# Storing each output of the last macro tile but one in two DMAs with 8 KB reads, in a rot90 kernel on Trainium2

## The chip, the cores and the metric

The kernel runs on one core of one Trainium2 chip. The metric is the device time of one execution in microseconds (us). Runs are compared with runs of the same rounds on the same chip. A run's time is about 1.8 us longer than the span that its trace covers.

Names: a *macro tile* is 1024 x 4096 floats of the input (16 MB). There are 16, so *tile 15* is the last but one and *tile 16* the last. Each is loaded by eight DMAs of 2 MB and leaves as eight *outputs* of 2 MB, numbered 0 to 7. *The turn* is the passage from the last load and the last output of tile 15 to the first output of tile 16. (MB and KB: 2 MB is 2,097,152 bytes; GB/s, and MB with a decimal point, are decimal.)

Engines, as this kernel uses them: PE transposes, DVE and ACT copy, SP issues the loads and ACT the stores. SBUF is the memory of the tiles; PSUM is the one that PE writes its results to. A *landing* is the end of a DMA, an *issue* the instruction that starts it.

## The reference

```python
def setup_inputs():
    return {"x": np.random.randn(8192, 8192).astype(np.float32), "k": 1}

def reference(x, k):
    return np.rot90(x, k)
```

268.4 MB are read and 268.4 MB are written. Nothing is computed; the work is to move and to turn.

## The kernel before

A load brings 128 rows x 4096 columns into SBUF. DVE reverses the columns inside each 128-wide block while copying to the reversal buffers `ar` (68 of them; one macro tile fills 64). PE transposes the 128 x 128 blocks into PSUM, 32 for one output, in two halves of 16. ACT copies each half to an output buffer `ot`, and issues the store. Pools: two load buffers, two output buffers, two PSUM tiles (each half an output).

```python
    a_pool = ctx.enter_context(tc.tile_pool(name="a_pool", bufs=2))
    r_pool = ctx.enter_context(tc.tile_pool(name="r_pool", bufs=68))
    o_pool = ctx.enter_context(tc.tile_pool(name="o_pool", bufs=2))
    psum_pool = ctx.enter_context(
        tc.tile_pool(name="psum", bufs=2, space=bass.MemoryType.PSUM)
    )
    # ... loads (SP queue) and DVE reversals, then for each output of the tile:
            if last and g0 // G % 2 == 0:
                ot = a_pool.tile([P, W], dt, tag="a")   # load buffers are free by then
            else:
                ot = o_pool.tile([P, W], dt, tag="o")
            o = ot.rearrange("m (g f) -> m g f", g=G)   # G = 4
            S = PW if last and g0 + G == C // P else G  # PW = 2
            for h in range(0, G, PW):
                ps = psum_pool.tile([P, PW, R], mybir.dt.float32)
                # ... 16 transposes into ps
                nc.scalar.copy(o[:, G - PW - h : G - h, :], ps[:])
                done = h + PW
                if done % S == 0:
                    # ... dst: S blocks of 128 rows x 1024 columns of out
                    nc.scalar.dma_start(out=dst, in_=o[:, G - done : G - done + S, :])
```

After scheduling, `whole_reads` rewrites the SBUF side of every store into one contiguous read for each partition. A 2 MB store thus reads 16 KB at a time, like a load. (Its HBM side still writes rows of 4 KB.) The profile shows these pieces as packets: it counts 144 for a 2 MB DMA, 18432 for the 128 loads, one for each of the 128 pieces and 16 of under 512 B (4112 of these in all 257 DMAs).

```python
                if len(ap) == 3 and ap[2][0] == 1 and ap[1][0] == ap[2][1]:
                    ap = [ap[0], [1, 1], [1, ap[1][1] * ap[2][1]]]
```

Of the kernel before, what the change touches and what calls it, by code (L numbers as in the profile page):

```python
# [2 lines left out]

# [5 lines left out]

P = 128  # L10




R = 1024
RT = R // P
LAST = [4096]
W = 4096
CH = 512
G = 4  # L20
PW = 2


def whole_reads(nc):






    for fn in nc.m.functions:
        for block in fn.blocks:
            for n, ins in enumerate(block.instructions):
                if not isinstance(ins, mybir.InstDMACopy):
                    continue
                src = ins.ins[0]
                ap = [list(d) for d in src.ap]
                if len(ap) == 3 and ap[2][0] == 1 and ap[1][0] == ap[2][1]:
                    ap = [ap[0], [1, 1], [1, ap[1][1] * ap[2][1]]]
                    block.instructions[n] = copy.replace(  # L40
                        ins,
                        ins=[copy.replace(src, ap=ap)],
                        ant_dge_precooked=False,
                    )


def macro_tiles(N, M):

    for r0 in range(0, N, R):
        widths = [W] * (M // W)  # L50
        if r0 + R == N:
            widths[-1:] = LAST
        c0 = 0
        for C in widths:
            yield r0, c0, C
            c0 += C


@with_exitstack
def kernel(  # L60
    ctx: ExitStack,
    tc: tile.TileContext,
    x: bass.AP,
    k: bass.AP,
    out: bass.AP,
):
    nc = tc.nc
    assert k == 1, f"only k=1 supported, got {k}"
    nc.at_finalize(whole_reads)

    N, M = x.shape
    dt = x.dtype

    consts = ctx.enter_context(tc.tile_pool(name="consts", bufs=1))
    ident = consts.tile([P, P], dt)
    make_identity(nc, ident)
# [8 lines that stand above are left out]
    tiles = list(macro_tiles(N, M))  # L85
    loads = 0
    for r0, c0, C in tiles:
        last = (r0, c0, C) == tiles[-1]
        q = W // C
        chunks = {}  # L90
        for t0 in range(0, RT, q):


            if loads < RT and loads % 4 >= 2:
                a = o_pool.tile([P, W], dt, tag="o")
            else:
                a = a_pool.tile([P, W], dt, tag="a")
            loads += 1
            a = a.rearrange("r (q c) -> r q c", q=q)
            nc.sync.dma_start(  # L100
                out=a,
                in_=x[r0 + t0 * P : r0 + (t0 + q) * P, c0 : c0 + C].rearrange(
                    "(q r) c -> r q c", q=q
                ),
            )


            for u in range(q):
                for j in range(C // CH):
                    ar = r_pool.tile([P, CH // P, P], dt, tag="ar")  # L110
                    nc.vector.tensor_copy(  # L111
                        out=ar[:],
                        in_=a[:, u, j * CH : (j + 1) * CH].rearrange(
                            "r (b m) -> r b m", m=P
                        )[:, :, ::-1],
                    )
                    chunks[t0 + u, j] = ar

        for g0 in range(0, C // P, G):

            if last and g0 // G % 2 == 0:
                ot = a_pool.tile([P, W], dt, tag="a")
            else:
                ot = o_pool.tile([P, W], dt, tag="o")
            o = ot.rearrange("m (g f) -> m g f", g=G)
            S = PW if last and g0 + G == C // P else G
            for h in range(0, G, PW):
                ps = psum_pool.tile([P, PW, R], mybir.dt.float32)
                for w in range(PW):
                    g = g0 + h + w  # L130
                    for t in range(RT):
                        nc.tensor.transpose(  # L132
                            ps[:, PW - 1 - w, t * P : (t + 1) * P],
                            chunks[t, g * P // CH][:, g % (CH // P), :],
                            ident,
# [5 lines that stand above are left out]
                    top = M - c0 - (g0 + done) * P  # L141
                    dst = out[top : top + S * P, r0 : r0 + R].rearrange(
                        "(g m) f -> m g f", g=S
                    )
                    nc.scalar.dma_start(  # L145
                        out=dst, in_=o[:, G - done : G - done + S, :]
                    )


# [1 line left out]
_INS = ['x', 'k']  # L151
_OUTS = [((8192, 8192), 'float32')]

_NUMBERS = {'k': 1}


# [26 lines left out]
```

## Time and profile before

| | before |
|---|---|
| time, median (lowest to highest) | 1271.75 us (1271.64 to 1271.89), 4 runs |
| span of the trace | 1269.2 us |
| PE / ACT / DVE busy | 56% / 37% / 28% |
| DMA, mean | 424 GB/s |

These lines are from the page of the profile: the busy tenths of the DMA engines and the rate, in 40 equal slices of the span; the chain that ended last, by line; and the DMA issues, with the median time from issue to landing as the last number.

```profile
...
DMA  9999999999999999999999999999999999999989
GB/s 400 415 431 429 429 428 429 430 428 429 428 429 428 430 430 428 429 429 430 428 428 420 429 429 429 429 429 427 428 422 427 426 421 430 427 427 427 428 342 382
...
DMA out_dram<-ot 72%; ACT ot L137 18%; DMA a<-in_x_dram 6%; DVE ar L111 1%; PE ps L132 1%; ACTq L145 0%; ACTq L137 0%; DVEq L111 0%
...
a<-in_x_dram SPq DMA_DIRECT2D x128, 2048.0 KB, 16.8
out_dram<-ot ACTq DMA_DIRECT2D x127, 2048.0 KB, 15.8
...
```

Nine tenths and more in every slice but one, at some 429 GB/s in most: the DMA engines bound the kernel. The slices that fall off are the last two. The timeline shows why. Its columns are start, duration, engine and line, operation, and in brackets how long the engine had been idle and what ended that; `x2` means that a line merges two instructions, and its duration runs from the start of the first to the end of the last. L137 is the ACT copy, L145 the store, L111 the DVE reversal, L132 the transposes.

```profile
...
1202.12 3.63 ACT L137 COPY ot<-ps 128x2048 f32<-128x2048 f32 x2 [6.19 <-DMA out_dram<-ot]
...
1211.95 3.63 ACT L137 COPY ot<-ps 128x2048 f32<-128x2048 f32 x2 [6.19 <-DMA out_dram<-ot]
...
1215.62 0.55 ACTq L145 DMA_DIRECT2D out_dram<-ot  x1
1218.09 2.77 DVE L111 COPY ar<-a 128x512 f32<-128x512 f32 x8 [7.05 <-DMA a<-in_x_dram]
...
1218.57 6.39 PE L132 MATMUL ps<-ident,ar 128*128 128x128 f32 x41 [3.72 <-DVE ar L111]
1220.79 1.87 ACT L137 COPY ot<-ps 128x2048 f32<-128x2048 f32 x1 [5.20 <-PE ps L132]
1223.25 1.87 ACT L137 COPY ot<-ps 128x2048 f32<-128x2048 f32 x1 [0.60 <-PE ps L132]
1225.15 0.55 ACTq L145 DMA_DIRECT2D out_dram<-ot  x1
...
```

The pace is 9.83 us for an output (1202.12 to 1211.95) as long as loads and stores run side by side. Then the last load lands and is reversed from 1218.09 on, and its transposes and the two ACT copies end at 1225.12. The first store of tile 16 is issued at 1225.15, when the last store of tile 15 (issued at 1215.62) is nearly out. The table of five-microsecond stretches of the same trace shows the hole. After the length come the busy us (and instructions) of PE, its weight loads, DVE, ACT and POOL; the last three columns are the granted TensorE clock, the busy share of the DMA engines, and GB/s.

```profile
...
1210.00:1215.00 5.00, 0.98 (x7) 0.74 (x7) 1.04 (x4) 3.05 (x2) 0.00 (x0) 1.00 0.90 382
1215.00:1220.00 5.00, 1.43 (x7) 1.43 (x8) 1.91 (x6) 0.59 (x1) 0.00 (x0) 0.53 0.80 338
1220.00:1225.00 5.00, 4.96 (x36) 4.72 (x34) 0.86 (x3) 3.61 (x2) 0.00 (x0) 0.79 0.34 144
1225.00:1230.00 5.00, 4.25 (x37) 3.97 (x38) 0.00 (x0) 3.76 (x3) 0.00 (x0) 1.00 0.74 315
...
```

Against 430 GB/s, these four stretches lose (48 + 92 + 286 + 115) x 5 / 430 = 6.3 us of transfer time. The change aims at this hole.

### The profile page before, as it was taken

Reading aid. Unit: us, or ns where it says so; the run is one execution under the profiler, and the core shown is the slowest. Engines: PE = TensorE matmul, PEld = TensorE weight load, DVE = VectorE, ACT = ScalarE, POOL = GpSimd, SP = SyncE. Lnnn points to the kernel's source line nnn. Section 1 sums busy time; section 2 is a strip of 40 time slices with the busy share of each in tenths; the row PEclk is TensorE's granted clock in tenths of the full one; section 3 lists DMA queues with packets and bytes.
Section 4 is the critical chain, followed back from the end, with each engine's and each line's share of the span. In section 5 each row is a group of like instructions: output and inputs, shape, how many; then the busy total and the mean of one; then the engine's idle time right before and its main releaser. Section 6 shows DMA issues by size and latency. Waiting matters only on the chain.

```text
span 1269.2 us, 10385 instructions
## 1 busy us (share of the span) xinstructions
PE 708.7 (56%) x4096; PEld 668.1 (53%) x4096; DVE 355.2 (28%) x1024; ACT 467.2 (37%) x257; POOL 0.7 (0%) x6
## 2 busy tenths in 40 slices
PE   1465645655556555665566555564555555655564
PEld 0364545645555455554556545554555555545564
DVE  4422322232223222232223222332223322232210
ACT  0333334333433343333433333333433343333454
POOL 0000000000000000000000000000000000000000
PEclk9968687776777867767767677677676877768787
DMA  9999999999999999999999999999999999999989
GB/s 400 415 431 429 429 428 429 430 428 429 428 429 428 430 430 428 429 429 430 428 428 420 429 429 429 429 429 427 428 422 427 426 421 430 427 427 427 428 342 382
DMA packets 37057, 537.55 MB, mean 424 GB/s; under 512 B 4112, under 2 KB 4112, under 8 KB 4112
## 3 DMA queue, kind: packets, MB, share of 16 engines
q10 hardware_dynamic: 18576, 268.44, 49.8%
q1 hardware_dynamic: 18432, 268.44, 49.8%
q8 instruction: 32, 0.52, 0.2%
q14 instruction: 17, 0.14, 0.0%
HBM read 268.44 MB, written 268.44 MB: 423 GB/s over the span
## 4 chain that ended last, share of the span: by engine, by line
DMA 78%; ACT 18%; DVE 1%; PE 1%; issue 1%; ACTq 0%; DVEq 0%
DMA out_dram<-ot 72%; ACT ot L137 18%; DMA a<-in_x_dram 6%; DVE ar L111 1%; PE ps L132 1%; ACTq L145 0%; ACTq L137 0%; DVEq L111 0%
## 5 line engine op out<-in xcount | busy, mean ns | idle before, releaser
L132 PE MATMUL ps<-ident,ar 128*128 128x128 f32 x4096 | 708.7, 353 | 544.3 <-ACT ot L137 461.5
L132 PEld LDWEIGHTS ps<-ident,ar 128*128 128x128 f32 x4096 | 668.1, 188 | 584.6 <-ACT ot L137 492.4
L137 ACT COPY ot<-ps 128x2048 f32<-128x2048 f32 x256 | 465.9, 1869 | 747.0 <-DMA out_dram<-ot 724.2
L111 DVE COPY ar<-a 128x512 f32<-128x512 f32 x1024 | 355.2, 421 | 865.7 <-DMA a<-in_x_dram 731.6
L137 ACT ACT_TABLE_LOAD x1 | 1.3, 1283 | 41.1 <-DVE ar L111 41.1
masks.py:199 POOL TENSOR_SCALAR_AFFINE_SELECT ident<-ident 128x128 f32<-128x128 f32 x1 | 0.3, 292 | 0.1
masks.py:197 POOL MEMSET ident<- 128x128 f32 x1 | 0.2, 204 | 0.3 <-POOLq L164 0.3
L164 POOL MEMSET const-bfloat16-1.0<- 128x1 bf16 x1 | 0.1, 101 | 0.0
L164 POOL MEMSET const-uint8-127<- 128x1 uint8 x1 | 0.1, 101 | 0.0
L164 POOL MEMSET const-float32-0.0<- 128x1 f32 x1 | 0.1, 98 | 0.2 <-issue 0.2
L164 POOL MEMSET const-float32-1.0<- 128x1 f32 x1 | 0.1, 98 | 0.0
## 6 DMA issues: line engine op xcount, KB each, us to landing
a<-in_x_dram SPq DMA_DIRECT2D x128, 2048.0 KB, 16.8
out_dram<-ot ACTq DMA_DIRECT2D x127, 2048.0 KB, 15.8
out_dram<-ot ACTq DMA_DIRECT2D x2, 1024.0 KB, 12.6
```

Of the source, the lines that this page charges most:

```text
L111: nc.vector.tensor_copy(out=ar[:], in_=a[:, u, j * CH : (j + 1) * CH].rearrange("r (b m) -> r b m", m=P)[:, :, ::-1],)
L132: nc.tensor.transpose(ps[:, PW - 1 - w, t * P : (t + 1) * P], chunks[t, g * P // CH][:, g % (CH // P), :], ident,)
L137: nc.scalar.copy(o[:, G - PW - h : G - h, :], ps[:])
L164: nc = _bacc.Bacc("TRN2", target_bir_lowering=False, num_devices=1)
```

## The change

The intent: give the loads of tile 16 a larger share of the DMA engines while tile 15 is being stored, so that they land early and the stores left over fill the hole.

```diff
+        ahead = (r0, c0, C) == tiles[-2]
...
-            S = PW if last and g0 + G == C // P else G
+            S = PW if ahead or (last and g0 + G == C // P) else G
```

The diff also removes the list `LAST = [4096]`, which had no effect. Each output of tile 15 now leaves in two 1 MB DMAs, whose SBUF reads are 8 KB instead of 16.

More of the change, by code (lines that the diff above doesn't have):

```diff
@@ L16 @@
 RT = R // P
-LAST = [4096]
 W = 4096
@@ L50, in macro_tiles @@
         widths = [W] * (M // W)
-        if r0 + R == N:
-            widths[-1:] = LAST
         c0 = 0
```

## The prediction

> **What bounds the kernel now.** The DMA engines. The page's forty slices show them 90% busy or more in all but one, at 427 to 430 GB/s in most; PE is busy 56%, ACT 37%, DVE 28%. 536.9 MB at 430 GB/s are 1249 us of the 1269 us span. The chain of waits shows the lockstep: landing of a store (15.8 us), two ACT copies (3.64 us), next store; with two output and two input buffers a 2 MB load and a 2 MB store pass in each 9.83 us.
>
> The change can reach only the loss at the turn into the last macro tile. In the timeline the last load's DVE copies start at 1218.1 us, the last store of the tile before is issued at 1215.6, and the first store of the last tile only at 1225.15, because transposes and two ACT copies lie between. The table of five-microsecond stretches from 1210 us shows 382, 338, 144, 315, 416 GB/s instead of 430: about 6.4 us of lost transfer time. The drain at the end (about 3 us) stays.
>
> **What the change does.** The eight 2 MB stores of the last macro tile but one become sixteen 1 MB stores with 8 KB SBUF reads. In the instruction order both halves are issued after the second ACT copy, so nothing starts earlier; eight more issues of 0.55 us fall on ACT, mostly in its waits. Bytes are the same; packets rise by about 1,150. [...] Then loads (16 KB) get two thirds and these stores (8 KB) one third. The trace of before shows no such share; it only mixes equal packets. So the last tile's loads run ahead of the stores, and the stores left over fill the gap while the last tile's first transposes and copies run.
>
> **How much comes back.** Not all. The last four chunks of each load need reversal buffers freed by the transposes of the matching output group (68 buffers, 64 in use), and these wait for ACT and so for slower stores. So the loads gain about one load's time: the last lands near 1209 instead of 1218 us. Then stores run alone with two buffers: between a landing and the next store's first bytes lie 3.64 us of ACT and about 3 us of latency (estimate: the first load landed at 8.1 us, where 2 MB at 430 GB/s take 4.9), more than the 4.9 us that the other buffer's 2 MB last. So a new dip of some 2 us opens. The last store of the tile before is issued near 1219 instead of 1215.6, the first of the last tile near 1223 instead of 1225. Stepping these durations through gives 1.5 us saved; the measured gap is deeper than in that sketch, so I say 2.2. [...]
>
> **Prediction: 1269.6 us**, 1266.0 to 1272.8. Chances: faster 0.01, within 2% 0.98, slower 0.01.
>
> **What would show it.** Issue to landing of the last eight loads falls from 16.8 to about 11 us at its shortest, and grows for the half stores. DVE then waits for PE in that tile. The dip of 144 GB/s at 1220 to 1225 us is partly filled, and another appears 5 to 10 us earlier. Before 1140 us nothing changes.
>
> **What would make it wrong.** Engines that share by bytes or by DMA, not by packets: no gain. A costly 8 KB packet: slower by 1 to 3 us. Loads held back less than I think: up to 5 us gained. [...]

The forecast of 1269.6 us is before's 1271.75 us less the 2.2 us saved. The shares were the author's assumption; they were measured afterwards (286 and 146 GB/s, below).

## The result

| | before | after |
|---|---|---|
| time, median (lowest to highest) | 1271.75 us (1271.64 to 1271.89) | 1271.47 us (1270.91 to 1271.85) |
| ratio, 95% interval | | 0.9997 (0.998 to 1.0015) |
| first store of tile 16 issued | 1225.15 us | 1226.09 us |
| time of the profiled run | 1270.97 us | 1271.85 us |

A ratio is the mean time of one kernel's runs over that of the other's of the same rounds, so it is not quite the ratio of the medians quoted. The time is the same within the noise. The time of 1271.47 lies in the predicted range, but that range (1266.0 to 1272.8) holds "no gain" as well as a gain, so this says little; the 2.2 us that were to come did not.

The page of the changed kernel, the lines that answer to those of before:

```profile
...
GB/s 398 415 432 429 428 429 428 430 428 429 428 429 430 428 429 428 428 429 430 429 429 426 426 429 427 428 429 427 428 426 428 425 426 429 428 426 413 395 368 382
...
DMA out_dram<-ot 47%; DMA a<-in_x_dram 31%; ACT ot L137 13%; DVE ar L109 5%; PE ps L132 1%; ACTq L145 0%; ACTq L137 0%; DVEq L109 0%
...
a<-in_x_dram SPq DMA_DIRECT2D x128, 2048.0 KB, 16.8
...
out_dram<-ot ACTq DMA_DIRECT2D x18, 1024.0 KB, 13.5
```

There are now 18 stores of 1 MB (two before), and the last four slices, not the last two, fall off. The timeline of tile 15's stores (ACT) and tile 16's loads (DVE; the reversal is L109 here):

```profile
...
1153.03 3.63 ACT L137 COPY ot<-ps 128x2048 f32<-128x2048 f32 x2 [6.26 <-DMA out_dram<-ot]
...
1157.68 2.77 DVE L109 COPY ar<-a 128x512 f32<-128x512 f32 x8 [5.52 <-DMA a<-in_x_dram]
1165.00 2.77 DVE L109 COPY ar<-a 128x512 f32<-128x512 f32 x8 [4.55 <-DMA a<-in_x_dram]
1167.77 3.63 ACT L137 COPY ot<-ps 128x2048 f32<-128x2048 f32 x2 [11.11 <-DMA out_dram<-ot]
...
1172.36 1.43 DVE L109 COPY ar<-a 128x512 f32<-128x512 f32 x4 [4.58 <-DMA a<-in_x_dram]
...
1182.11 3.63 ACT L137 COPY ot<-ps 128x2048 f32<-128x2048 f32 x2 [10.71 <-DMA out_dram<-ot]
...
```

Loads now land 7.3 us apart (1157.68, 1165.00, 1172.36), which is 2.10 MB / 7.34 us = 286 GB/s, two thirds of 430. Before it was one in 9.83 us. Outputs go the other way: ACT's waits for a store to land end 14.7 and 14.3 us apart (1153.03, 1167.77, 1182.11), 2.10 / 14.34 = 146 GB/s, one third. On average over this stretch the predicted share is there. The `x4` and the later groups of the same kind show DVE stopping half way through a load. Waits from 1140 us on (engine and tile, what it waited for, total us, times, longest), first before:

```profile
...
DVE ar L111 <- DMA a<-in_x_dram: 56.5, 8, 7.1
...
```

and after:

```profile
...
DVE ar L109 <- DMA a<-in_x_dram: 34.1, 7, 7.2
DVE ar L109 <- PE ps L132: 21.6, 5, 7.6
...
```

Before, DVE waited for loads alone. After, 21.6 us of its waiting is for PE to free reversal buffers: the loads have run as far ahead as they can. Now the turn, after:

```profile
...
1210.36 1.43 DVE L109 COPY ar<-a 128x512 f32<-128x512 f32 x4 [2.99 <-DMA a<-in_x_dram]
1211.59 3.63 ACT L137 COPY ot<-ps 128x2048 f32<-128x2048 f32 x2 [8.59 <-DMA out_dram<-ot]
...
1213.51 8.09 PE L132 MATMUL ps<-ident,ar 128*128 128x128 f32 x48 [6.84 <-ACT ot L137]
1217.22 1.86 ACT L137 COPY ot<-ps 128x2048 f32<-128x2048 f32 x1 [2.00 <-PE ps L132]
...
1219.88 1.87 ACT L137 COPY ot<-ps 128x2048 f32<-128x2048 f32 x1 [0.80 <-PE ps L132]
1219.94 2.38 ACTq L145 DMA_DIRECT2D out_dram<-ot  x2
...
1222.42 3.63 ACT L137 COPY ot<-ps 128x2048 f32<-128x2048 f32 x2 [0.67 <-ACT ot L137]
...
1226.09 0.55 ACTq L145 DMA_DIRECT2D out_dram<-ot  x1
...
```

and the stretches of the same trace:

```profile
...
1210.00:1215.00 5.00, 1.49 (x7) 1.49 (x8) 1.43 (x4) 3.41 (x2) 0.00 (x0) 0.50 0.70 295
1215.00:1220.00 5.00, 5.00 (x30) 5.00 (x29) 0.88 (x3) 2.21 (x3) 0.00 (x0) 0.61 0.96 398
1220.00:1225.00 5.00, 4.21 (x37) 3.74 (x36) 0.55 (x2) 4.33 (x3) 0.00 (x0) 1.00 0.82 338
1225.00:1230.00 5.00, 4.41 (x41) 4.14 (x39) 0.00 (x0) 4.30 (x3) 0.00 (x0) 1.00 0.84 352
...
```

The last load is being reversed at 1210.36 instead of 1218.09, as intended, and the stretch of 144 GB/s is gone. But outputs 6 and 7 are late: the copies of output 7, at 1211.95 before, come at 1217.22 and 1219.88, and the second half of its store goes out at 1221.78 (the second issue of 1219.94, 2.38 long). Tile 16 follows directly behind, and its first store is issued at 1226.09, 0.94 us later than before. Instead of one deep hole there are several shallow ones. Summed over 1170 to 1230 us, the time lost against 430 GB/s was 6.5 us before and 7.6 after, although the engines' idle share in it fell from 6.2 to 4.2 us.

### The profile page after: what moved, and what is told of

It is laid out like the page before. It is cut to its first block, busy times and chain, and to the rows that moved or that the text cites. A ratio compares the mean times of both kernels' runs of the same rounds, so it can differ in the third digit from the quotient of the medians.

```text
span 1270.1 us, 10398 instructions
## 1 busy us (share of the span) xinstructions
PE 706.6 (56%) x4096; PEld 666.8 (53%) x4096; DVE 355.4 (28%) x1024; ACT 467.4 (37%) x257; POOL 0.7 (0%) x6
## 4 chain that ended last, share of the span: by engine, by line
DMA 78%; ACT 13%; DVE 5%; PE 1%; issue 1%; ACTq 0%; DVEq 0%
DMA out_dram<-ot 47%; DMA a<-in_x_dram 31%; ACT ot L137 13%; DVE ar L109 5%; PE ps L132 1%; ACTq L145 0%; ACTq L137 0%; DVEq L109 0%
## 5 line engine op out<-in xcount | busy, mean ns | idle before, releaser
L109 DVE COPY ar<-a 128x512 f32<-128x512 f32 x1024 | 355.4, 421 | 865.1 <-DMA a<-in_x_dram 751.4
## 6 DMA issues: line engine op xcount, KB each, us to landing
a<-in_x_dram SPq DMA_DIRECT2D x128, 2048.0 KB, 16.8
```

Of the source, the lines that this page charges most:

```text
L109: nc.vector.tensor_copy(out=ar[:], in_=a[:, u, j * CH : (j + 1) * CH].rearrange("r (b m) -> r b m", m=P)[:, :, ::-1],)
```

## The experiments

Kernels are compared only within the same rounds. Times are medians of five or six runs. The kernel before spread more in these rounds (1268.4 to 1272.3 us in all) than in the first, so differences under about 1 us are not resolved.

### Packet size or number of DMAs

Theory P: the size of a store's reads sets the shares. Rival D: more and smaller DMAs do it. The first run has the packets of after and the number of DMAs of before.

```diff
                     ap = [ap[0], [1, 1], [1, ap[1][1] * ap[2][1]]]
+                    if 112 <= store < 120:      # the eight stores of tile 15
+                        ap = [ap[0], [2048, 2], [1, 2048]]
+                    store += 1
```

> The kernel before, with the eight stores of the last macro tile but one kept as single 2 MB DMAs but read in 8 KB pieces of SBUF (packets as after, number of DMAs as before). Theory P (the packet size alone sets the share of the two queues): the same picture as after. Loads of the last tile land early (shortest issue to landing near 11 us), DVE waits for PE in that tile, the last load's first DVE copies start near 1210 us instead of 1218.1, time 1270.9 to 1272.3 us. Rival D (more and smaller DMAs do it): the picture of before, last load at 1218 us, 144 GB/s at 1220 to 1225 us, time 1271.7.

Measured: 1272.61 us against 1271.45, ratio 1.001 (0.9998 to 1.0022). Timeline:

```profile
...
1158.03 2.77 DVE L115 COPY ar<-a 128x512 f32<-128x512 f32 x8 [5.54 <-DMA a<-in_x_dram]
1165.65 2.78 DVE L115 COPY ar<-a 128x512 f32<-128x512 f32 x8 [4.84 <-DMA a<-in_x_dram]
...
1212.72 1.43 DVE L115 COPY ar<-a 128x512 f32<-128x512 f32 x4 [7.42 <-DMA a<-in_x_dram]
...
```

Loads land 7.6 us apart (1158.03, 1165.65), shortest issue to landing 11.4 us (11.1 in after, 16.7 before), the last load is reversed from 1212.72. This is the picture of after with before's number of DMAs, so the size of the reads is sufficient by itself. P holds for the shares (275 GB/s for the loads and 149 for the stores, from landings 7.62 and 14.08 us apart); the time is 0.3 us above the range given for it, and the last load comes 2.7 us later than its 1210.

The counterpart has two DMAs for each output, of 64 partitions each, with 16 KB reads:

```diff
+                    parts = [(0, 64), (64, 128)] if ahead else [(0, P)]
+                    for p0, p1 in parts:
-                    nc.scalar.dma_start(out=dst, in_=o[:, G - done : G - done + S, :])
+                        nc.scalar.dma_start(out=dst[p0:p1], in_=o[p0:p1, ...])
```

> The kernel before, with the eight stores of the last macro tile but one split into two 1 MB DMAs by partitions (0 to 63, 64 to 127), so that the reads stay 16 KB (number of DMAs as after, packets as before). Theory P: the picture of before, last load's copies at 1218 us, gap at 1220 to 1225 us, time 1271.7 within 0.4 us. Rival D: the picture of after, last load near 1210 us.

Measured: 1276.80 us, ratio 1.0046 (1.0034 to 1.0058): slower by about 5 us, which neither theory expected. Loads do not run ahead (issue to landing 17.0 us at the shortest), so D falls. But it is not the clean control that was meant:

```profile
...
1174.23 3.63 ACT L138 COPY ot<-ps 128x2048 f32<-128x2048 f32 x2 [6.86 <-DMA out_dram<-ot]
...
1184.59 3.63 ACT L138 COPY ot<-ps 128x2048 f32<-128x2048 f32 x2 [6.73 <-DMA out_dram<-ot]
...
```

The pace in tile 15 is 10.4 us here (10.4 to 11.2 from 1152.58 us on) instead of 9.83, at 388 to 405 GB/s, in stretches of 10 us between 1175 and 1205 us, with the engines fully busy (busy share 0.98 to 1.01). Six outputs, from the copies at 1152.58 us to those at 1216.69, take 64.1 us instead of 6 x 9.83 = 59.0: 5.1 us more, about the whole difference, or some 0.6 us for each of the eight outputs.

### What the small packets cost in steady state

Every 2 MB store of the whole kernel with 8 KB reads, loads at 16 KB:

```diff
+                    if ap[2][1] == 4096:
+                        ap = [ap[0], [2048, 2], [1, 2048]]
```

> Every 2 MB store of the whole kernel read in 8 KB pieces, loads at 16 KB. If the share is by packets, loads run ahead all the time until the reversal buffers stop them, as in the last tile but one of after; its cost is then repeated in all 16 tiles. Theory C (8 KB store packets beside 16 KB loads lose rate: 3.4 us in after's window 1170 to 1230 us were busy but slow): 10 to 50 us slower than before, 1282 to 1320 us. Rival F (the packets cost nothing, only the end counts): 1270 to 1274 us.

Measured: 1307.33 us, ratio 1.0275 (1.024 to 1.031). The waits over the whole run:

```profile
...
DVE ar L113 <- PE ps L134: 495.0, 89, 10.2
DVE ar L113 <- DMA a<-in_x_dram: 404.1, 90, 8.7
...
```

DVE waited longer for PE than for loads: the loads come to the limit of the reversal buffers again and again (89 such waits for 128 loads), then outputs catch up in bursts, then loads again, with stretches at 291 and 360 GB/s where the queues change over (614 to 616 and 616 to 618 us, busy share 0.93 and 0.92). The loss is (1307.33 - 1271.45) / 128 = 0.28 us for each output.

Is it the small packet itself? The run has 8 KB reads on both sides (for a load, its SBUF side too), so that the shares are equal:

```diff
+                if len(ap) == 2 and ap[1] == [1, 4096]:      # a load: both sides
+                    # ... source and destination as [.., [2048, 2], [1, 2048]]
```

> Loads and stores both in 8 KB packets in the whole kernel, equal again, so no load runs ahead. Theory C in the form 'an 8 KB packet itself is slower': period over 9.83 us in steady state, 1% to 3% slower, 1284 to 1310 us. Rival 'only unequal packets or queues running dry cost': the picture of before, 1271 to 1274 us.

Measured: 1279.69 us, ratio 1.0067 (1.0055 to 1.0079). That is 8.24 / 128 = 0.064 us for each output with its load, 0.7%, even though the loads have small packets as well. It lies between the two expectations: not free (the rival said 1271 to 1274 us), but under the 1% of theory C. Loads keep their 16.8 us from issue to landing. So of the 0.28 us an output, at least 0.22 are put down, by subtraction, to unequal shares and not to the packet. If the eight outputs of tile 15 pay what the average output of that kernel pays, this makes an estimate of 8 x 0.22 = 1.7 us, worked out from these two runs, that the run-ahead gives back before the turn. No run measures that part by itself.

### A shorter stretch of halves

Theory T: the unequal share helps at the turn alone and costs as long as it lasts, so a shorter stretch should win. Rival G: the share is worth nothing to the end.

```diff
-            S = PW if ahead or (last and g0 + G == C // P) else G
+            S = PW if (ahead and g0 >= 4 * G) or (last and ...) else G   # last four
+            S = PW if (ahead and g0 >= 6 * G) or (last and ...) else G   # last two
```

> After, but only the last four of the eight outputs of the last macro tile but one are stored in halves. Theory T (run-ahead is useful only at the turn; while the loads are stopped by the reversal buffers one queue runs dry and rate is lost, so a shorter stretch loses less): DVE's waits for PE shrink, busy-but-slow loss falls from 3.4 us to about half, time 1270.0 to 1271.0, below after's 1271.5. Rival G (the share is worth nothing to the end whatever its length): 1271.5 within 0.3.

> After, but only the last two of the eight outputs are stored in halves. Theory T: hardly any DVE wait for PE, last load at 1214 to 1217 us, idle dip at 1220 to 1225 us partly filled, time 1269.5 to 1270.5 us, the fastest of after, the last-four kernel and this one. Rival G: 1271.5 within 0.3 us.

Measured, before in the same rounds 1270.66: last four 1268.76, ratio 0.9984 (0.9971 to 0.9996); last two 1269.83, ratio 0.9991 (0.9979 to 1.0004). DVE's wait for PE is 0.9 us and none. So G falls: the last-four kernel gains 1.9 us by the medians, about what the change was predicted to gain (T expected 1270.0 to 1271.0 us). The 0.8 us of the last-two kernel are not resolved. T had the last two in front of the last four, which is wrong.

The last three (`g0 >= 5 * G`) and the changed kernel once more:

> After with only the last three of the eight outputs in halves. Theory T (useful at the turn alone, harmful while the reversal buffers stop the loads): between the last-four kernel (1.9 us below before) and the last-two one (0.8 to 1.1 us below): 1.2 to 2.0 us below before. Rival G: within 0.3 us of before.

> The changed kernel itself once more, unedited, on the chip of the runs beside it, so that the shorter stretches are compared with it in the same rounds. Expected: 1270.5 to 1271.9 us, within 0.5 us of before, while last-three and last-four halves are 1.5 to 2.3 us below before.

Measured, before in the same rounds 1270.81: after again 1271.20, ratio 1.0002 (0.9989 to 1.0014); last three 1270.73, ratio 0.9999 (0.9985 to 1.0013). The last three gain nothing, though four, one more, gain 1.9 us. T as stated is refuted: it is not the length of the stretch alone that counts. The timelines of the turn tell the two apart. Last four:

```profile
...
1214.83 3.63 ACT L137 COPY ot<-ps 128x2048 f32<-128x2048 f32 x2 [4.46 <-PE ps L132]
...
1216.75 3.73 PE L132 MATMUL ps<-ident,ar 128*128 128x128 f32 x32 [1.57 <-ACT ot L137]
1219.13 3.64 ACT L137 COPY ot<-ps 128x2048 f32<-128x2048 f32 x2 [0.67 <-PE ps L132]
...
1222.80 0.55 ACTq L145 DMA_DIRECT2D out_dram<-ot  x1
...
```

Last three:

```profile
...
1215.10 3.64 ACT L137 COPY ot<-ps 128x2048 f32<-128x2048 f32 x2 [9.28 <-DMA out_dram<-ot]
...
1217.02 7.69 PE L132 MATMUL ps<-ident,ar 128*128 128x128 f32 x48 [7.53 <-ACT ot L137]
1220.73 1.87 ACT L137 COPY ot<-ps 128x2048 f32<-128x2048 f32 x1 [2.00 <-PE ps L132]
...
1224.90 0.55 ACTq L145 DMA_DIRECT2D out_dram<-ot  x1
...
```

(The 4.46 us of wait before output 7 are put down to PE, whose first 16 transposes were over by then; in the version with DVE below, the same wait, 4.47 us, is put down to the landing of an earlier store, which fits.) In the last-four kernel PE has hardly paused before tile 16 (1.57 us); its 32 transposes take 3.73 us, and ACT goes from output 7 (1214.83) into tile 16 (1219.13) without a wait that costs. In the last-three kernel output 7 comes at nearly the same time (1215.10), but PE had waited 7.53 us, 48 transposes take 7.69 us, and ACT waits 2.00 us for them. The first store of tile 16 is issued at 1224.90 instead of 1222.80, and the end differs by the same 2 us.

The same comparison for the profiled runs of all kernels whose tile 16 is that of before, sorted by the issue of tile 16's first store:

| kernel | first store of tile 16 | time of that run | difference |
|---|---|---|---|
| last four | 1222.80 | 1268.76 | 45.96 |
| last two | 1224.36 | 1270.34 | 45.98 |
| last three | 1224.90 | 1270.97 | 46.07 |
| after, 71 buffers (below) | 1224.93 | 1270.73 | 45.80 |
| before | 1225.15 | 1270.97 | 45.82 |
| after, again | 1225.31 | 1271.20 | 45.89 |
| after | 1226.09 | 1271.85 | 45.76 |
| one DMA, 8 KB reads | 1226.20 | 1272.61 | 46.41 |
| two DMAs by partitions | 1226.80 | 1276.80 | 50.00 |

(The difference holds the 1.8 us by which a run's time exceeds its trace.) In all but the last row the end comes 45.8 to 46.4 us after the first store of tile 16, whatever happened in tile 15. The exception has its stores so far behind that the engines do not run dry at the turn (idle share 0.6 us from 1170 to 1230 us, against 6.2 before); tile 16 then queues behind bytes still owed, as I read it from that share. Wherever the engines do run dry, the question for a change of this kind is when that store goes out.

### Is it the reversal buffers that stop the loads?

71 buffers are the most that the build accepts; with 72 it stops for want of space (32 KB for each partition asked for the output buffers, 31.3 KB left). Edit: `bufs=68` to `bufs=71` in the changed kernel.

> After with 71 reversal buffers instead of 68 (the most that fit), all eight outputs in halves. If the buffers are what stops the loads from running ahead, DVE's waits for PE after 1140 us fall from 21.6 us to under 15 us and the time falls by 0.3 to 1.0 us against after. If the buffers do not matter: waits and time as after.

Measured: 1271.06 us, ratio 1.0003 (0.9991 to 1.0016), no gain. From 1140 us on DVE still waits 20.8 us for PE (21.6 in the first profile of after, 25.2 in the second). Three buffers do not shift it. That PE frees what DVE waits for is read from the waits; that more buffers would pay is not shown, and there is no room to try.

### Only the first store of tile 16 earlier

On the kernel before, output 0 of tile 16 is stored in two halves; or copied and stored in four quarters as its transposes finish.

```diff
-            S = PW if last and g0 + G == C // P else G
+            S = PW if last and g0 in (0, C // P - G) else G                        # halves
+            S = 1 if last and g0 == 0 else PW if last and g0 + G == C // P else G  # quarters
...             (with S == 1, each block is copied and stored inside the loop)
```

> Before, with the first output of the last macro tile stored in two halves, so that its first 1 MB leaves after one ACT copy instead of two. If the gap at the turn is latency between the last load and the first store, the first store is issued at 1222.7 instead of 1225.15 us and the time falls by 2 to 2.5 us, to 1269.3 us. If the gap is not on the critical path: 1271.7 us.

> Before, with the first output of the last macro tile copied and stored in four quarters of 512 KB, each after its eight transposes. Latency theory: first store issued near 1220.7 instead of 1225.15 us, time down by 3.5 to 4.5 us, to 1267.3 to 1268.2 us. If the gap is off the critical path: 1271.7 us.

Measured against 1270.66: halves 1271.08, ratio 1.0000 (0.9986 to 1.0014); quarters 1270.55, ratio 0.9996 (0.9984 to 1.0009). Both missed. The first bytes did leave earlier (first half issued at 1223.16, first quarter at 1219.89), but output 1 did not follow in time: its store was issued at 1229.30 and 1228.11, against 1229.46 before. ACT needs 4.31 us for an output (1230.13 to 1234.44 before), while the engines need 4.9 us for 2 MB at 430 GB/s. An estimate from these two: as output 1 is ready 4.31 us after output 0, starting output 0 early, alone, can gain at most 4.9 - 4.3 = 0.6 us. After that the engines run dry again, which the traces show (277 and 203 GB/s in the quarters kernel from 1226 to 1230 us). The whole train of tile 16 has to come earlier, which is what the last-four kernel does. This also corrects the table's rule: in these two kernels the end comes 47.1 and 49.3 us after the first bytes of tile 16, so the rule holds for the first store together with those behind it.

### A version that beats both

Last four in halves; in tile 16, output 0 in halves, the second half of each later output copied by DVE (which is idle by then: 0.00 us busy from 1225 to 1255 us before), and the stores issued from SP.

```diff
+            S = PW if (ahead and g0 >= 4 * G) or (last and g0 in (0, C // P - G)) else G
...
+                if last and g0 > 0 and h > 0:
+                    nc.vector.tensor_copy(out=o[:, G - PW - h : G - h, :], in_=ps[:])
+                else:
                     nc.scalar.copy(o[:, G - PW - h : G - h, :], ps[:])
...
-                    nc.scalar.dma_start(
+                    (nc.sync if last else nc.scalar).dma_start(
```

> Last-four halves, and in the last macro tile the first output stored in halves, every later output copied half by ACT and half by DVE, and its stores issued from SP. If the ACT pace (4.31 us per output) after the turn is what kept the earlier first store from counting (halves and quarters of the first output gained 0 to 0.5 us), outputs now come every 3.7 to 4.0 us and the time falls to 1.0 to 2.0 us below the last-four kernel, 3 to 4 us below before. If the DMA engines alone limit the last tile: as last-four, 1.9 us below before.

Measured: 1268.20 us (1267.95 to 1268.29) against 1270.81, ratio 0.9978 (0.9966 to 0.9991). It is the fastest kernel, 2.6 us under before by the medians, less than the 3 to 4 us expected. Against last-four (ratio 0.9984) the intervals overlap, so what DVE adds is not shown.

## Why the prediction was right or wrong

**What bounds the kernel: right.** The DMA engines (busy nine tenths and more in 39 of 40 slices), and the hole at the turn, 6.3 us deep.

**The share by packets: right, on average.** "Loads (16 KB) get two thirds and these stores (8 KB) one third": 286 and 146 GB/s, from landings 7.3 and 14.3 us apart. That it is the size of the pieces and not the number of DMAs is shown by the run with one DMA and 8 KB reads (275 and 149 GB/s). How the engines come to these shares is not shown. In slices of one microsecond the pieces come in bursts: before the change, at 1153 us, the trace has 4 packets of loads and 23 of stores, and at 1157 us 23 and 6. The bursts last some 5 us, and a whole DMA of 2 MB would take 4.9 us at the trace's 430 GB/s (an estimate). But turns of one whole DMA do not fit: in the run with one DMA and 8 KB reads, loads and stores are 2 MB each, which would make the shares equal. What ends a turn stays open.

**How far the loads get: right.** "The last lands near 1209": it is reversed from 1210.36. "About 11 us at its shortest": 11.1. "DVE then waits for PE in that tile": 21.6 us of such waits.

**"In the instruction order both halves are issued after the second ACT copy, so nothing starts earlier": wrong.** The trace has the first half's issue of output 0 at 1145.03 us, when the first copy (from 1143.13, 1.87 us) is just over, and that of output 7 at 1219.94, just after the second copy starts (1219.88), not after it ends (1221.75). So the first half leaves nearly one copy earlier than the prediction had it. No run shows what that was worth.

**The last store of tile 15 "near 1219", the first of the last tile "near 1223 instead of 1225": wrong, and this is the step that failed.** The second half of the last store of tile 15 was issued at 1221.78, and the first store of tile 16 at 1226.09 (1225.31 in the repeat). Since the end follows 46 us behind that train, the saving of 2.2 us became nothing (medians 0.28 us apart). The distance between the two stores is as predicted (4.3 us instead of 4); what is late is output 7. The prediction counts between two stores a landing, 3.64 us of ACT and some latency, but no wait for PE. In after, ACT waited 2.00 and 0.80 us for PE before and between the two copies of output 7, and 1221.78 less these 2.8 us is 1219.0. So the term left out of the sum is a wait of 2.8 us for PE.

Most of that wait comes with slow transposes. At a granted clock of 1.00 (1225 to 1230 us) 16 of them take 1.97 us (at 1225.18 before), and ACT then waits 0.67 us once in an output. At the turn of after, PE had waited 6.84 us for ACT, the granted clock was 0.50 from 1210 to 1215 us, and the first 16 of output 7 took 3.7 us (1213.51 to 1217.22, when the copy of their half starts). At full clock, then, some 2.1 of the 2.8 us would not have been there (an estimate from these waits). In steady state before, the same slow clock (0.50 from 1155 to 1160 us) is hidden, because ACT waits 6.2 us for a landing anyway. The change removed that wait at the turn and laid the PE time bare.

When the clock was slow is read from the traces. At the turn the first 16 transposes took 3.7 us after pauses of PE of 6.84, 7.53 and 4.06 us (after, last three, 71 buffers), with a granted clock of 0.50, 0.50 and, on average, 0.56 in the five microseconds that hold their start; after 1.57 and 2.48 us (last four, and the version with DVE) 32 took 3.73 us at 1.00, the full clock. In the last-two kernel seven slow transposes (1.76 us) came after a pause of 4.45 us; the 41 that follow 1.42 us later begin slow too (0.50 from 1215 to 1220 us), and take 7.00 us. Pauses of about 4 us go either way: seven transposes just before the turn took 0.98 us after a pause of 3.99 us in before, which is full clock (1.00 from 1210 to 1215 us), and 1.76 us after 3.93 us in the run with the first output in halves. Of the kernels whose loads run ahead, the two with the full clock there are also the two that gained 1.9 us or more. That is a reading of traces: no run took the slow clock away by itself, so it is not shown by an experiment that it alone made the difference. When the outputs before output 7 land has a part in it too (ACT waited 4.46 us before output 7 in last four, 9.28 in last three), and that shifts with the number of halves in a way that I did not foresee.

**What 8 KB reads cost was not in the sum.** They cost 0.7% where loads and stores both have them (1279.69 against 1271.45 us). And unequal shares cost in steady state something I had not counted: 0.22 us an output by the two whole-kernel runs, an estimate of 1.7 us over tile 15. The traces show stretches of low rate with busy engines when the queues change over (291 and 360 GB/s, above).

## What to carry to other kernels

The size of a DMA's contiguous pieces is a lever on how two queues share the engines (286 and 146 GB/s with 16 and 8 KB here); here it paid only for a few transfers just ahead of the moment at which one queue must be ahead (1.9 us by the medians with four outputs), and in steady state unequal shares cost rate (an estimate of 0.22 us an output). When a change removes a wait, cost what lay hidden behind it at the speed that it will have there: here 16 transposes took 3.7 us at a granted clock of 0.50, after PE had paused 6.84 us, instead of 1.97 us. And at a turn where the engines run dry, the whole train behind has to come earlier, not its first transfer alone.
